# Weight forms and returned chunks of a streaming encoder layer ordered by the scheduler, and other buffer turns in its gate-pair stage

## The chip, the cores and the metric

The kernel runs on one core of a Trainium2 chip. A core has a matrix engine (TensorE, PE in the profile, with PEld for its weight loads), VectorE (DVE), ScalarE (ACT), GpSimd (POOL) and SyncE (SP), whose queue issues most of the transfers. Each engine works through its own list of instructions and waits for others by semaphores. The metric is the time of one execution in microseconds (us); less is better.

## The reference

One layer of a streaming encoder with two parallel mixers, on 2048 prompt rows and 64 new rows of a running stream that has 4096 rows in a cache:

```python
h = rmsnorm(x, norm_g)
q, k, v, ga, u, gb, mg = split(h @ w_in)            # 8 heads of 128; w_in is 1024 x 8192
z = einsum('bqhd,bkhd->bhqk', q, k) * 128 ** -0.5
log_beta = log_sigmoid(z)                           # stick-breaking attention, strictly causal
log_1m = where(mask, log_beta - z, 0)
after = cumsum(log_1m, reverse=True) - log_1m
att = where(mask, exp(log_beta + after), 0) @ v
pb = multi_scale_pool(u) * pool_scale               # trailing means over 2, 4, 8, 16 rows
y_a = (att * silu(ga)) @ w_br_a
y_b = (pb * silu(gb)) @ w_br_b
gate = sigmoid(mg)                                  # 2 x 1024 columns
x = x + (gate[:, :1024] * y_a + gate[:, 1024:] * y_b) @ w_out
y = rmsnorm(x, final_g)                             # returned with k, v and the pool's rows
```

All is float32.

## The kernel before

**Products.** Each float32 operand is split into two parts that TensorE takes fast: `hi` is a rounded copy (a cast on ACT, L91), `lo` is the rest (a subtraction on DVE, L92). A product is three matmuls: hi by hi, hi by lo, lo by hi. So a column slab of 128 weights needs a *form* ahead of its projection (`load_w`): two raw loads of 256 KB by SP (`raw`, three buffers, L310), and two cast-and-subtract pairs into `whi` and `wlo` (two buffers each).

**Attention.** The prompt is worked in two halves of 1024 rows. In the second half, each of the 8 heads (0 to 7) has 28 *units* of 128 query rows by up to 512 key rows. A unit's chain is: scores on PE (L804 to L806), two sigmoids on ACT (`om` L734, `be` L735), for diagonal units a causal select on POOL (L719), a running product from the right on DVE (the scan, L742), the product `be` with it (L745), transposes on PE (`tr`, L818), the split of `tr` into `a` hi and lo (L91, L92), and the products with the values on PE (L833 to L835). Four units make a block; a block's first transpose group reads the `be` of all four. At step n, PE runs the scores of unit n, the transposes of unit n−4 and the products of unit n−5. Between these steps PE works at the four projection slabs (K, V, Q, gate) of the next head, so head 7 has no slabs beside it. The keys and values of the first half come back from memory for each head (`kback`, `vback`) as 2 chunks each, and are split too; each head's own new keys and values are split after their projection (`kst`, `nat`).

**Who sets the order.** PE runs in the order in which the program is written, throughout. ACT, DVE and SP run in written order in the front, in the gate-pair stage and in the closing stage. In the stage of the heads a scheduler orders them, but an instruction given to `keep_in_program_order` stays where the program has it. `placed_split` (L339 to L341) does this for a split. Before, three things in the heads of the second half are placed so: the weight forms, by a hook in the projections that does one half of a form at the 3rd and one at the 6th of every 8 steps (`form_ahead`); the returned chunks, at fixed units (`k` at units 1 and 3, `v` at 7 and 9); and the split of the second own values chunk (`late_v`), at unit 2.

**The gate-pair stage** follows the heads (from L1378 on). Pairs of gate columns are computed by seven products each, p = 0 to 6, on sums of blocks. The accumulators are `z` for even p and `att` for odd p; after p = 0, 2 and 3 the accumulator is copied to `gx` by ACT (`gate_keep`, L1419), and p = 4 overwrites nothing before that copy is done. The weights of the first pair are formed by `stream_forms` (the generator `prepare`, in turns of `whi` and `wlo`), those of later pairs by `pair_forms` from `graw` (loads L1390, differences L1406, L1407, L1411, L1414). Between products runs `weight_sums`, which loads blocks of two other weight matrices by POOL's queue into tiles `ws`, subtracts them and stores the differences (`tw_d`). Its tiles share the buffers of `whi` and `wlo`:

```python
ts = [pool.tile([P, KT, P], F32, name="ws", tag=tag, bufs=2) for tag in ("whi", "wlo")]
```

**The closing stage** computes the two branch products and the output in the same way of seven products. It reads the differences (`wraw<-tw_d`, forms `t1`, `t2`, ...), and the gates that were stored as `sm_d` (`sg<-sm_d`).

Of the kernel before, what the change touches and what calls it, by code (L numbers as in the profile page):

```python
# [8 lines left out]
F32 = mybir.dt.float32  # L9
# [6 lines left out]
P = 128  # L16
# [29 lines left out]
def kernel(  # L46
# [118 lines left out]
    with ExitStack() as front:  # L165
# [161 lines left out]
        def form_w(spare=False):  # L327
            if spare:
                return [attp.tile([P, KT, P], F32R, name=nm, tag="a", bufs=2) for nm in ("wqhi", "wqlo")]
            return [pool.tile([P, KT, P], F32R, name=nm, tag=nm, bufs=2) for nm in ("whi", "wlo")]  # L330
# [5 lines left out]
                split(whi[:, k:k + 4], wlo[:, k:k + 4], raw_w(col, k), eng)  # L336
            return whi, wlo

        def placed_split(hi, lo, src):  # L339
            tc.keep_in_program_order(nc.scalar.copy(hi, src))  # L340
            tc.keep_in_program_order(nc.vector.tensor_tensor(lo, src, hi.bitcast(F32), op=ALU.subtract))  # L341

        cols_ahead, forms_ahead, part_of, steps_of = [], {}, [], [0]

        def form_ahead():
            n = steps_of[0] % 8
            steps_of[0] += 1
            if n == 1 and cols_ahead:
                col = cols_ahead.pop(0)
                forms_ahead[col] = form_w()  # L350
                part_of.extend((forms_ahead[col], k, raw_w(col, k)) for k in range(0, KT, 4))
            elif n in (2, 5) and part_of:
                (hi, lo), k, raw = part_of.pop(0)
                placed_split(hi[:, k:k + 4], lo[:, k:k + 4], raw)

        def proj_ahead(groups, slab):
            col = slab[0]
            yield from proj(groups, [slab], None, [forms_ahead.pop(col)] if col in forms_ahead else (), form_ahead)

        def proj(groups, slabs, eng=None, ws=(), hook=None):  # L360


            ws = list(ws) + [load_w(col, eng, n == 2) for n, (col, _) in enumerate(slabs) if n >= len(ws)]
            for g, (c0, n) in enumerate(groups):
                for (whi, wlo), (_, evac) in zip(ws, slabs):
                    ps = psum.tile([P, 512], F32, name="pj")
                    for k in range(KT):
                        nc.tensor.matmul(ps[:, 0:n], whi[:, k], hhi[:, k, c0:c0 + n], start=k == 0, stop=False)  # L368
                        nc.tensor.matmul(ps[:, 0:n], whi[:, k], hlo[:, k, c0:c0 + n], start=False, stop=False)  # L369
                        nc.tensor.matmul(ps[:, 0:n], wlo[:, k], hhi[:, k, c0:c0 + n], start=False, stop=k == KT - 1)  # L370
                        if k == KT - 1:
                            evac(g, c0, n, ps)
                        if k % 2:
                            if hook:
                                hook()
                            yield 6 * mm_ns(n)

        def groups_of(half):
# [209 lines left out]
                return 107.0  # L588
            defer(2500, rows)

        placed, loaded = {}, {}

        def head_proj(half, hd, fine=False, ws=()):
            groups = groups_of(half)
            col = hd * P
# [34 lines left out]

            def evac_v(g, c0, n, ps):
                st, npr, c, o = staged(g, c0, n, ps)
                late_v = half and not fine and c
                if o == 0 and not late_v:
                    out["v"][c0h + c] = vchunk()

                def rows():
                    r0 = half * 1024 + c0
                    nat = natural(st[:, 0:npr], npr, [vp[r0:r0 + npr, hd, :]])
                    if late_v:  # L640
                        placed.setdefault(hd, []).append((2, out["v"], c0h + c, vchunk, nat))
                    else:
                        vhi, vlo = out["v"][c0h + c]
                        split(vhi[:, o:o + npr], vlo[:, o:o + npr], nat[:, 0:npr], "v" if fine else None)
                    spill("v", c, o, nat[:, 0:npr])
                    if npr < n:
                        later_rows(st[:, npr:n], [vsm[:, hd, :], sv_d[hd]])
                    return npr * 0.85
                defer(6500 if fine else 2500, rows)
# [50 lines left out]
                return  # L700
            if fine:
                yield from proj(FINE_B, [(OFF_K + col, evac_k), (OFF_V + col, evac_v), (OFF_Q + col, evac_q)], None, ws)
                if half:
                    cols_ahead.extend(o + h * P for h in range(1, H) for o in (OFF_K, OFF_V, OFF_Q, OFF_GA))
            else:
                one = proj_ahead if half else lambda groups, slab: proj(groups, [slab])
                yield from one(groups, (OFF_K + col, evac_k))
                yield from one(groups, (OFF_V + col, evac_v))
                yield from one(groups, (OFF_Q + col, evac_q))
            if half:  # L710
                yield from proj_ahead(groups, (OFF_GA + col, evac_g))
            else:
                yield from proj(groups, [(OFF_GA + col, evac_g)])
            heads[half, hd] = out


# [35 lines left out]
        class Stream:  # L752
# [27 lines left out]
            def scores(self, n):  # L780
                hd, qb, c, i = self.units[n]
                out = heads[self.half, hd]
                diag = c == qb
                todo = placed.setdefault(hd, [])
                for cc in range(2 * self.half - 1, -1, -1):
                    if cc in loaded.setdefault(hd, []):
                        continue
                    loaded[hd].append(cc)
                    for kind, chunk in (("k", kchunk), ("v", vchunk)):
                        raw = attp.tile([P, 512], F32, name=f"{kind}back", tag=f"{kind}raw", bufs=2)  # L790
                        nc.sync.dma_start(raw, kvd[kind, hd, cc])
                        todo.append(({"k": 3, "v": 9}[kind] - 2 * cc, out[kind], cc, chunk, raw))
                todo.sort(key=lambda x: x[0])
                while todo and n % 28 >= todo[0][0]:
                    _, of, cc, chunk, raw = todo.pop(0)
                    of[cc] = chunk()
                    placed_split(*of[cc], raw)
                khi, klo = out["k"][c]
                qhi, qlo = out["q"][qb]
                m = P * (i + 1) if diag else 512  # L800
                off = 512 - m
                z = psum.tile([P, 512], F32, name="z")
                qs = slice(i * P, (i + 1) * P)
                nc.tensor.matmul(z[:, off:512], qhi[:, qs], khi[:, 0:m], start=True, stop=False)  # L804
                nc.tensor.matmul(z[:, off:512], qhi[:, qs], klo[:, 0:m], start=False, stop=False)  # L805
                nc.tensor.matmul(z[:, off:512], qlo[:, qs], khi[:, 0:m], start=False, stop=True)  # L806
                om = self.om or self.complements(n)
                be, self.carry[i] = weights_of_block(z, off, om, diag, ahead=lambda: self.prepare(n + 1))
                self.be[hd, qb, c, i] = (be, off)
                return 3 * mm_ns(m) + self.lead(n)  # L810
# [638 lines left out]
        forms_of = pair_forms()  # L1449

        closing_sums = weight_sums()
        next(closing_sums)
        with tc.manual_schedule(engines={E.Activation, E.DVE, E.SP}):
            for c in range(*GATE_PAIRS, 2):
                x = psum.tile([P, 512], F32, name="z")
# [92 lines left out]
        def before_closing():  # L1548
# [32 lines left out]
            for nm, b in (("r21", 0), ("r22", 1)):  # L1581
                for h, t in enumerate(whole_rows(nm, 1, b)):
                    rows(t, 1, b, h)
            yield from todo

        last_gates = [proj(GROUPS_B, [merge_gate(1, c)], ws=ahead_w if c == GATE_PAIRS[1] else ())
                      for c in range(GATE_PAIRS[1], 2 * KT)]
        run((before_closing(), 12.0), (chain(*last_gates), 1.6 * slab_ns(1)))
# [104 lines left out]
    with tc.manual_schedule(engines={E.PE, E.DVE, E.Activation, E.SP}):  # L1693
# [93 lines left out]
        for i, base, nms, at in ((0, 0, WFORMS[3:], [1, 2, 5, 6, 7, 8, 9, 10]),  # L1787
                                 (1, 28, WFORMS, [30 + (8 * h) // 5 for h in range(14)]),
                                 (2, 70, WFORMS[:6], [71 + h for h in range(10)] + [85, 86])):
            when.setdefault(base, []).append((i, nms))  # L1790
            for h in at:
                when.setdefault(h, []).append(None)
        sums_at = {11: 0, 15: 1, 18: 2, 59: 3}
# [9 lines left out]
                pending.append(sums_step(2, sums_at[h]))  # L1803

        pending = []
        wnext = [None]
        for n in range(3):
            load_gate(n)
        for ks in halves:
# [331 lines left out]
```

## Time and profile before

| | before |
|---|---|
| median of 3 runs | 2691.92 us (2687.89 to 2696.8) |
| the profiled execution's own time | 2688.06 us |
| its span (first to last instruction) | 2686.1 us |
| TensorE's granted clock, mean | 0.999 |
| PE busy | 2660.3 us (99%) |
| DVE busy | 1914.1 us (71%) |
| ACT busy | 1327.1 us (49%) |
| POOL busy | 418.2 us (16%) |
| memory traffic over the span | 126 GB/s |

In the rows of the trace the first number is the start in us from the span's start, the second the length in us, then the engine, the line, the operation and its tiles as output<-inputs. A bracket at the end gives the idle time of the engine just before the instruction and what ended it. In a row of the waits the numbers are the total in us, how often, and the longest. The instructions are numbered by the lines of the kernel before; the kernel after has the same code some 30 to 40 lines higher up (the scan L742 is L707, the multiplication L745 is L710).

### The profile page before, as it was taken

The numbers are of one execution on the slowest core, as the hardware profiler recorded it, in microseconds if no ns is written. First come the engines' busy times: TensorE is split into PE (matmuls) and PEld (weight loads), VectorE is DVE, ScalarE is ACT, GpSimd is POOL, SyncE is SP. The second block draws the span as 40 slices with busy tenths as digits, with TensorE's granted clock in tenths as the row PEclk, the third lists the DMA queues.
The fourth block names the chain that finished last, engine by engine and source line by source line (L and its number), as shares of the span: only waits on it lengthen the run. The fifth ranks groups of instructions, "written<-read, shape, count | busy, mean of one in ns | idle before, by whom it ended". The sixth has DMA issues, their size and how long they took to land.

```text
span 2686.1 us, 42384 instructions
## 1 busy us (share of the span) xinstructions
PE 2660.3 (99%) x15066; PEld 2343.0 (87%) x15066; DVE 1914.1 (71%) x3028; ACT 1327.1 (49%) x2627; POOL 418.2 (16%) x1202
## 2 busy tenths in 40 slices
PE   9999999999999999999999999999999999999998
PEld 8999999988899989988888888888887889999886
DVE  5555555567777784488888888888956757677877
ACT  5446444455555553365556656665433443332443
POOL 1122222220000000021212222131000301111001
PEclk9999999999999999999999999999999999999999
DMA  4224222234444444212111211211344868687753
GB/s 149 85 82 131 75 74 74 80 98 153 149 153 152 157 151 157 88 56 60 44 48 55 60 37 55 59 39 49 118 138 148 285 222 297 227 290 249 261 176 119
DMA packets 338706, 342.45 MB, mean 127 GB/s; under 512 B 29799, under 2 KB 281055, under 8 KB 338494
## 3 DMA queue, kind: packets, MB, share of 16 engines
q1 hardware_dynamic: 324382, 293.87, 34.7%
q0 software_dynamic: 14112, 45.89, 4.7%
q8 instruction: 118, 1.93, 0.3%
q14 instruction: 94, 0.77, 0.1%
HBM read 231.02 MB, written 108.65 MB: 126 GB/s over the span
## 4 chain that ended last, share of the span: by engine, by line
PE 90%; DVE 5%; issue 2%; ACT 1%; DMA 1%; POOL 1%; SPq 0%; POOLq 0%; DVEq 0%; ACTq 0%
PE pj L368 15%; PE pj L369 15%; PE pj L370 15%; PE tr L818 4%; PE x L1598 3%; PE x L1600 3%; PE x L1602 3%; PE y L1598 3%; PE y L1600 3%; PE y L1602 3%; PE att L835 2%; PE z L806 2%; DVE om L742 2%; PE z L805 2%; PE att L834 2%
## 5 line engine op out<-in xcount | busy, mean ns | idle before, releaser
L368 PE MATMUL pj<-hhi,whi 128*128 128x256 f32 (+2 forms) x2288 | 817.6, 357 | 0.0
L370 PE MATMUL pj<-hhi,wlo 128*128 128x256 f32 (+2 forms) x2288 | 791.2, 346 | 0.0
L369 PE MATMUL pj<-hlo,whi 128*128 128x256 f32 (+2 forms) x2288 | 790.9, 346 | 0.3 <-DVE hlo L1071 0.3
L742 DVE TENSOR_TENSOR_SCAN om<-om 128x513 f32<-128x513 f32 (+3 forms) x356 | 390.8, 1098 | 200.5 <-POOL om L719 100.3
L370 PEld LDWEIGHTS pj<-hhi,wlo 128*128 128x128 f32 x2288 | 431.2, 188 | 50.6
L368 PEld LDWEIGHTS pj<-hhi,whi 128*128 128x128 f32 x2288 | 432.7, 189 | 46.1 <-ACT hhi L1068 0.3
L369 PEld LDWEIGHTS pj<-hlo,whi 128*128 128x128 f32 x2288 | 432.4, 189 | 44.1 <-DVE hlo L1071 0.5
L734 ACT ACTIVATE om<-z 128x512 f32<-128x512 f32 (+2 forms) x320 | 171.2, 535 | 285.5 <-PE z L806 255.1
L745 DVE TENSOR_TENSOR be<-be,om 128x512 f32<-128x512 f32 (+3 forms) x356 | 218.7, 614 | 33.1 <-POOL carry L744 0.5
L92 DVE TENSOR_TENSOR a<-tr,a 128x512 fp32r<-128x512 f32 (+2 forms) x356 | 215.8, 607 | 27.3 <-ACT a L91 25.2
L91 ACT CAST a<-tr 128x512 fp32r<-128x512 f32 (+2 forms) x356 | 188.0, 528 | 91.7 <-PE tr L818 83.3
L744 POOL COPY carry<-om 128x1 f32<-128x1 f32 x356 | 72.5, 204 | 860.4 <-DVE om L742 834.5
L92 DVE TENSOR_TENSOR wlo<-raw,whi 128x512 fp32r<-128x512 f32 x169 | 115.4, 688 | 96.4 <-ACT whi L91 95.7
L818 PE MATMUL tr<-ident,be 128*128 128x128 f32 x1088 | 174.1, 273 | 7.2 <-DVE be L745 6.6
L818 PEld LDWEIGHTS tr<-ident,be 128*128 128x128 f32 x1088 | 135.9, 140 | 40.7 <-DVE be L745 10.4
L735 ACT ACTIVATE be<-z 128x512 f32<-128x512 f32 (+2 forms) x320 | 169.4, 529 | 0.0
L91 ACT CAST whi<-raw 128x512 fp32r<-128x512 f32 x172 | 106.4, 623 | 95.8 <-PE pj L369 75.0
L833 PE MATMUL att<-a,v 128*128 128x512 f32 (+1 forms) x320 | 132.8, 415 | 0.0
L835 PE MATMUL att<-a,v 128*128 128x512 f32 (+1 forms) x320 | 118.3, 370 | 0.5 <-DVE a L92 0.2
L806 PE MATMUL z<-khi,qlo 128*128 128x512 f32 (+2 forms) x320 | 117.0, 366 | 0.0
L834 PE MATMUL att<-a,v 128*128 128x512 f32 (+1 forms) x320 | 116.4, 364 | 0.0
L805 PE MATMUL z<-klo,qhi 128*128 128x512 f32 (+2 forms) x320 | 116.4, 364 | 0.0
(528 smaller groups left out, 5244.4 us busy)
## 6 DMA issues: line engine op xcount, KB each, us to landing
raw<-in_w_in_dram SPq DMA_DIRECT2D x230, 256.0 KB, 3.0
sg<-sm_d SPq DMA_DIRECT2D x48, 352.0 KB, 5.8
kraw<-in_cache_k_dram SPq DMA_DIRECT2D x64, 256.0 KB, 3.2
vraw<-in_cache_v_dram SPq DMA_DIRECT2D x64, 256.0 KB, 3.1
sm_d<-sgm SPq DMA_DIRECT2D x48, 256.0 KB, 3.3
wraw<-tw_d SPq DMA_DIRECT2D x22, 512.0 KB, 4.0
out_dram<-nat SPq DMA_DIRECT2D x42, 256.0 KB, 2.3
mp_d<-sg POOLq DMA_DIRECT2D x24, 352.0 KB, 4.6
```

The source lines that it names most:

```text
L91: nc.scalar.copy(hi, src)
L92: (nc.gpsimd if eng == "g" else nc.vector).tensor_tensor(lo, src, hi.bitcast(F32), op=ALU.subtract)
L368: nc.tensor.matmul(ps[:, 0:n], whi[:, k], hhi[:, k, c0:c0 + n], start=k == 0, stop=False)
L369: nc.tensor.matmul(ps[:, 0:n], whi[:, k], hlo[:, k, c0:c0 + n], start=False, stop=False)
L370: nc.tensor.matmul(ps[:, 0:n], wlo[:, k], hhi[:, k, c0:c0 + n], start=False, stop=k == KT - 1)
L734: nc.scalar.activation(om[:, off:512], z[:, off:512], AF.Sigmoid, scale=-SCALE)
L742: nc.vector.tensor_tensor_scan(rev, rev, rev, 1.0, op0=ALU.mult, op1=ALU.bypass)
L745: nc.vector.tensor_tensor(be[:, off:512], be[:, off:512], om[:, off + 1:513], op=ALU.mult)
L805: nc.tensor.matmul(z[:, off:512], qhi[:, qs], klo[:, 0:m], start=False, stop=False)
L806: nc.tensor.matmul(z[:, off:512], qlo[:, qs], khi[:, 0:m], start=False, stop=True)
L818: nc.tensor.transpose(tr[:, i * P:(i + 1) * P], be[:, off + j * P:off + (j + 1) * P], ident)
L835: nc.tensor.matmul(self.acc[:, s], vhi[:, js], alo[:, s], start=False, stop=last)
```

## The change

Three things change; no instruction is added or removed, and PE's and POOL's orders stay the same.

1. In the heads of the second half nothing is placed any more. Weight forms go through `load_w` at the start of a slab's projection in the program, the own values are split where they are made, and the returned chunks are split where they are loaded, and the scheduler finds all of them a place.
2. The call `next(closing_sums)` ahead of the pair loop is gone, so each step of `weight_sums` comes one call later, and its first tiles `ws` take their turn of the `whi` and `wlo` buffers after the last form of `stream_forms` instead of before it.
3. The forms of `t1` and what follows it are begun at the end of `before_closing`, so their first two loads of 512 KB stand on SP's queue ahead of the last two gate stores `sm_d<-sgm` and of the first gate loads `sg<-sm_d`.

```diff
-        def placed_split(hi, lo, src):
-            tc.keep_in_program_order(nc.scalar.copy(hi, src))
-            tc.keep_in_program_order(nc.vector.tensor_tensor(lo, src, hi.bitcast(F32), op=ALU.subtract))
...
-        def form_ahead():
-            n = steps_of[0] % 8
...
-            elif n in (2, 5) and part_of:
-                (hi, lo), k, raw = part_of.pop(0)
-                placed_split(hi[:, k:k + 4], lo[:, k:k + 4], raw)
-
-        def proj_ahead(groups, slab):
...
-        def proj(groups, slabs, eng=None, ws=(), hook=None):
+        def proj(groups, slabs, eng=None, ws=()):
...
                 def rows():
                     r0 = half * 1024 + c0
                     nat = natural(st[:, 0:npr], npr, [vp[r0:r0 + npr, hd, :]])
-                    if late_v:
-                        placed.setdefault(hd, []).append((2, out["v"], c0h + c, vchunk, nat))
-                    else:
-                        vhi, vlo = out["v"][c0h + c]
-                        split(vhi[:, o:o + npr], vlo[:, o:o + npr], nat[:, 0:npr], "v" if fine else None)
+                    split(vhi[:, o:o + npr], vlo[:, o:o + npr], nat[:, 0:npr], "v" if fine else None)
...
-                        todo.append(({"k": 3, "v": 9}[kind] - 2 * cc, out[kind], cc, chunk, raw))
-                todo.sort(key=lambda x: x[0])
-                while todo and n % 28 >= todo[0][0]:
-                    _, of, cc, chunk, raw = todo.pop(0)
-                    of[cc] = chunk()
-                    placed_split(*of[cc], raw)
+                        out[kind][cc] = chunk()
+                        split(*out[kind][cc], raw)
...
         closing_sums = weight_sums()
-        next(closing_sums)
         with tc.manual_schedule(engines={E.Activation, E.DVE, E.SP}):
...
             yield from todo
-
+            wnext[0] = forms(0, WFORMS[3:], True)
+            next(wnext[0])
+
+        wnext = [None]
...
-            when.setdefault(base, []).append((i, nms))
+            if i:
+                when.setdefault(base, []).append((i, nms))
```

Where the orders differ, on DVE, at three places. In the rows the names are `om` (the scan's tile), `be`, `a`, `klo` and `v` (lo parts of chunks), `wlo` (lo part of weights), `qlo`; a number behind a name is the tile's.

The first place: DVE in a steady head, from unit 2's scan to unit 3's multiplication. Before:

```order
L742 SCALAR_TENSOR_TENSOR om_15806<-om_15806 128x385
L745 TENSOR_TENSOR be_15838<-be_15838,om_15806 128x384
L92 TENSOR_TENSOR a_15856<-tr_15851,a_15856 128x512
L89 CAST khi_15870<-kst_15868 128x512
L92 TENSOR_TENSOR klo_15871<-kst_15868,khi_15870 128x512
L341 TENSOR_TENSOR klo_15875<-kback_15740,khi_15874 128x512
L742 SCALAR_TENSOR_TENSOR om_15845<-om_15845 128x513
L92 TENSOR_TENSOR a_15900<-tr_15895,a_15900 128x512
L745 TENSOR_TENSOR be_15882<-be_15882,om_15845 128x512
```

After:

```order
L707 SCALAR_TENSOR_TENSOR om_15813<-om_15813 128x385
L710 TENSOR_TENSOR be_15840<-be_15840,om_15813 128x384
L92 TENSOR_TENSOR a_15858<-tr_15853,a_15858 128x512
L89 CAST khi_15872<-kst_15870 128x512
L92 TENSOR_TENSOR klo_15873<-kst_15870,khi_15872 128x512
L707 SCALAR_TENSOR_TENSOR om_15847<-om_15847 128x513
L92 TENSOR_TENSOR a_15898<-tr_15893,a_15898 128x512
L710 TENSOR_TENSOR be_15880<-be_15880,om_15847 128x512
```

The subtraction of the returned keys has left the place ahead of unit 3's scan.

The second place: DVE in the same head, around units 22 to 24. Before:

```order
L92 TENSOR_TENSOR a_16598<-tr_16595,a_16598 128x256
L341 TENSOR_TENSOR wlo_16577<-raw_16578,whi_16576 128x512
L742 SCALAR_TENSOR_TENSOR om_16589<-om_16589 128x513
L92 TENSOR_TENSOR a_16627<-tr_16625,a_16627 128x128
L745 TENSOR_TENSOR be_16616<-be_16616,om_16589 128x512
L742 SCALAR_TENSOR_TENSOR om_16619<-om_16619 128x513
L745 TENSOR_TENSOR be_16637<-be_16637,om_16619 128x512
L682 TENSOR_TENSOR sga_16652<-pj_16539,sga_16652 128x512
L92 TENSOR_TENSOR a_16660<-tr_16655,a_16660 128x512
```

After:

```order
L92 TENSOR_TENSOR a_16595<-tr_16592,a_16595 128x256
L707 SCALAR_TENSOR_TENSOR om_16586<-om_16586 128x513
L92 TENSOR_TENSOR a_16622<-tr_16620,a_16622 128x128
L710 TENSOR_TENSOR be_16611<-be_16611,om_16586 128x512
L92 TENSOR_TENSOR klo_16764<-kback_16761,khi_16763 128x512
L707 SCALAR_TENSOR_TENSOR om_16614<-om_16614 128x513
L653 TENSOR_TENSOR sga_16647<-pj_16542,sga_16647 128x512
L710 TENSOR_TENSOR be_16632<-be_16632,om_16614 128x512
L92 TENSOR_TENSOR v_16254<-nat_16284,v_16254 128x512
L92 TENSOR_TENSOR a_16655<-tr_16650,a_16655 128x512
```

A weight subtraction has left, and a keys' subtraction of the next head and the own values' subtraction now stand ahead of the last `a`.

The third place: DVE in head 0, units 22 and 23. Before:

```order
L742 SCALAR_TENSOR_TENSOR om_14466<-om_14466 128x513
L745 TENSOR_TENSOR be_14493<-be_14493,om_14466 128x512
L92 TENSOR_TENSOR qlo_14509<-pj_14405,qhi_14508 128x512
L92 TENSOR_TENSOR a_14515<-tr_14512,a_14515 128x256
L742 SCALAR_TENSOR_TENSOR om_14496<-om_14496 128x513
L745 TENSOR_TENSOR be_14525<-be_14525,om_14496 128x512
L92 TENSOR_TENSOR a_14543<-tr_14541,a_14543 128x128
```

After:

```order
L707 SCALAR_TENSOR_TENSOR om_14459<-om_14459 128x513
L710 TENSOR_TENSOR be_14486<-be_14486,om_14459 128x512
L92 TENSOR_TENSOR wlo_14737<-raw_14738,whi_14736 128x512
L92 TENSOR_TENSOR qlo_14502<-pj_14400,qhi_14501 128x512
L92 TENSOR_TENSOR a_14508<-tr_14505,a_14508 128x256
L707 SCALAR_TENSOR_TENSOR om_14489<-om_14489 128x513
L92 TENSOR_TENSOR wlo_14737<-raw_14742,whi_14736 128x512
L710 TENSOR_TENSOR be_14518<-be_14518,om_14489 128x512
L92 TENSOR_TENSOR a_14546<-tr_14544,a_14546 128x128
```

Two weight subtractions of the next head now stand in unit 23's chain, one ahead of `qlo` and one between scan and multiplication.

More of the change, by code (lines that the diff above doesn't have):

```diff
@@ L337, in load_w @@
             return whi, wlo
-        def placed_split(hi, lo, src):
-            tc.keep_in_program_order(nc.scalar.copy(hi, src))
-            tc.keep_in_program_order(nc.vector.tensor_tensor(lo, src, hi.bitcast(F32), op=ALU.subtract))
-        cols_ahead, forms_ahead, part_of, steps_of = [], {}, [], [0]
-        def form_ahead():
-            n = steps_of[0] % 8
[L347 to L351, printed above, removed]
-            elif n in (2, 5) and part_of:
-                (hi, lo), k, raw = part_of.pop(0)
-                placed_split(hi[:, k:k + 4], lo[:, k:k + 4], raw)
-        def proj_ahead(groups, slab):
-            col = slab[0]
-            yield from proj(groups, [slab], None, [forms_ahead.pop(col)] if col in forms_ahead else (), form_ahead)
-        def proj(groups, slabs, eng=None, ws=(), hook=None):
+        def proj(groups, slabs, eng=None, ws=()):
             ws = list(ws) + [load_w(col, eng, n == 2) for n, (col, _) in enumerate(slabs) if n >= len(ws)]
@@ L373, in proj @@
                         if k % 2:
-                            if hook:
-                                hook()
                             yield 6 * mm_ns(n)
@@ L589, in later_rows @@
             defer(2500, rows)
-        placed, loaded = {}, {}
         def head_proj(half, hd, fine=False, ws=()):
@@ L632, in evac_v @@
                 st, npr, c, o = staged(g, c0, n, ps)
-                late_v = half and not fine and c
-                if o == 0 and not late_v:
+                if o == 0:
                     out["v"][c0h + c] = vchunk()
+                vhi, vlo = out["v"][c0h + c]
                 def rows():
@@ L702, in head_proj @@
                 yield from proj(FINE_B, [(OFF_K + col, evac_k), (OFF_V + col, evac_v), (OFF_Q + col, evac_q)], None, ws)
-                if half:
-                    cols_ahead.extend(o + h * P for h in range(1, H) for o in (OFF_K, OFF_V, OFF_Q, OFF_GA))
-            else:
[L706 to L713, printed above, removed]
+            else:
+                yield from proj(groups, [(OFF_K + col, evac_k)])
+                yield from proj(groups, [(OFF_V + col, evac_v)])
+                yield from proj(groups, [(OFF_Q + col, evac_q)])
+            yield from proj(groups, [(OFF_GA + col, evac_g)])
             heads[half, hd] = out
@@ L783, in scores @@
                 diag = c == qb
-                todo = placed.setdefault(hd, [])
                 for cc in range(2 * self.half - 1, -1, -1):
-                    if cc in loaded.setdefault(hd, []):
+                    if cc in out["k"]:
                         continue
-                    loaded[hd].append(cc)
                     for kind, chunk in (("k", kchunk), ("v", vchunk)):
@@ L1805 @@
         pending = []
-        wnext = [None]
         for n in range(3):
```

## The prediction

> **What bounds the kernel now.** I read the page's busy times first, then what ended TensorE's waits, then single stretches in order of time.
>
> ```profile
> span 2686.1 us, 42384 instructions
> ...
> PE 2660.3 (99%) x15066; PEld 2343.0 (87%) x15066; DVE 1914.1 (71%) x3028; ACT 1327.1 (49%) x2627; POOL 418.2 (16%) x1202
> ```
>
> TensorE (PE) is busy for 2660.3 of 2686.1 us, so all of its idle time is 25.8 us. Its work and order stay as they are, so no edit here can gain more than 25.8. A loss has no such lid: every late input becomes idle time.
>
> The waits of PE come next: us in total, times, longest.
>
> ```profile
> PE tr L818 <- DVE be L745: 6.6, 11, 1.5
> PE z L1230 <- ACT gx L1419: 3.0, 1, 3.0
> ...
> PE att L1230 <- ACT whi L91: 0.5, 1, 0.5
> ```
>
> The first row is in the attention: a transpose waits for the weights `be` that VectorE (DVE) multiplies at L745. The other two stand in the pair stage, once each. The change touches both. The stretches of one steady head of the second half, of the last head and of the first follow.
>
> ```profile
> 1600.10:1693.50 93.40, 92.76 (x478) 76.95 (x477) 76.88 (x106) 55.99 (x113) 21.24 (x74) 1.00 0.17 52
> 1787.00:1870.00 83.00, 80.85 (x408) 66.36 (x407) 71.05 (x98) 49.19 (x98) 21.19 (x68) 1.00 0.16 51
> 1137.00:1226.00 89.00, 88.45 (x450) 72.53 (x449) 74.31 (x102) 52.64 (x106) 19.20 (x74) 1.00 0.17 51
> ```
>
> The columns are the length, then busy time of PE, weight load, DVE, ScalarE (ACT) and GpSimd (POOL), then the granted clock. In a steady head PE idles 0.64 us of 93.4, while DVE is busy for 76.9: 16.5 us are free on DVE, but it matters where they lie. Only every fourth unit's multiplication is urgent, because a block's first transpose needs the `be` of all four of its units. There are six steady heads.
>
> **The change part by part.** *Steady heads, unit 3.* One head, in order of time:
>
> ```profile
> 1322.32 0.30 POOL L719 TENSOR_SCALAR_AFFINE_SELECT om<-om 128x128 f32<-128x128 f32 x1 [2.69 <-ACT om L734]
> ...
> 1328.04 0.62 ACT L340 CAST khi<-kback 128x512 fp32r<-128x512 f32 x1
> ...
> 1328.56 0.59 ACT L734 ACTIVATE om<-z 128x512 f32<-128x512 f32 x1
> ...
> 1328.60 0.69 DVE L92 TENSOR_TENSOR klo<-kst,khi 128x512 fp32r<-128x512 f32 x1
> ...
> 1329.21 0.68 DVE L341 TENSOR_TENSOR klo<-kback,khi 128x512 fp32r<-128x512 f32 x1
> 1329.22 0.82 POOL L719 TENSOR_SCALAR_AFFINE_SELECT om<-om 128x128 f32<-128x128 f32 x1 [1.28 <-ACT om L734]
> ...
> 1330.08 1.29 DVE L742 TENSOR_TENSOR_SCAN om<-om 128x513 f32<-128x513 f32 x1 [0.19 <-POOL om L719]
> ...
> 1331.88 0.68 DVE L745 TENSOR_TENSOR be<-be,om 128x512 f32<-128x512 f32 x1
> ...
> 1332.61 0.33 PE L818 MATMUL tr<-ident,be 128*128 128x128 f32 x1 [0.63 <-DVE be L745]
> ```
>
> The chain into the transpose that waits 0.63 is: ACT `om`, POOL select, DVE scan, DVE multiplication. The change takes the cast of the returned keys (0.62 of sequence on ACT, 0.52 between the two starts 1328.04 and 1328.56) and its subtraction (two starts on DVE 0.61 apart) out of this place. With `om` about 0.5 earlier, the select starts about 0.5 earlier; it still meets `klo<-kst`, which holds DVE to 1329.29. A select beside no such subtraction took 0.30 (1322.32), the one here 0.82. So the scan starts at about 1329.5 in place of 1330.08, and the wait of 0.63 nearly goes. I take −0.55 per head, between 0 (the select is as late as now) and −0.75 (the idle time with the slow restart behind it). Six heads: −3.3, ends 0 and −4.5. What is late next is the scan behind its `om`, with no margin to spare.
>
> The row for the select is where a rule bears: the Trainium skill, SBUF — State Buffer, section "SBUF: two separate sides", says that DVE reading two SBUF inputs and GpSimd share a port by an exclusive lock, and that the one that loses is blocked fully. By that rule the select waits until `klo<-kst` ends and the gain stays 0.55; with no lock it would be the 0.75. The trace agrees with the lock, 0.82 against 0.30.
>
> *Steady heads, unit 24.* The subtractions that left unit 3 and its neighbour now stand late in the head before. The same order, at this place before:
>
> ```profile
> 1398.84 1.22 DVE L742 TENSOR_TENSOR_SCAN om<-om 128x513 f32<-128x513 f32 x1
> ...
> 1400.16 0.69 DVE L745 TENSOR_TENSOR be<-be,om 128x512 f32<-128x512 f32 x1
> ...
> 1401.37 0.68 DVE L92 TENSOR_TENSOR a<-tr,a 128x512 fp32r<-128x512 f32 x1
> ...
> 1402.48 0.40 PE L835 MATMUL att<-a,v 128*128 128x512 f32 x1
> ```
>
> Now one `klo` and one `v` subtraction stand ahead of `a`, at 0.6 each: 1.2 later. Before, `a` ends at 1402.05 and PE needs it at 1402.48, 0.43 of margin. The cost is 1.2 − 0.43 = 0.77; I take 0.7, since one weight subtraction leaves just ahead of it, between 0 (the scan waits for its `om` anyway and the `klo` hides in that wait) and 1.2. Six heads: +4.2, ends 0 and +7.2. The ACT casts of both pieces move along and hide under ACT's 40% of free time.
>
> *The weight forms.* They now stand as pairs of subtractions in four places per head in place of eight single ones. Where one is urgent, at unit 7:
>
> ```profile
> 1343.81 0.69 DVE L745 TENSOR_TENSOR be<-be,om 128x512 f32<-128x512 f32 x1
> ...
> 1345.85 0.60 PE L818 MATMUL tr<-ident,be 128*128 128x128 f32 x4
> ```
>
> `be` ends at 1344.50 and PE comes at 1345.85: 1.35 of margin. One more subtraction of 0.6 leaves 0.75, two leave 0.15. I cost this at 0; the cover is that margin, and the slower rival below is the case without it. Net of the steady heads: −3.3 + 4.2 = +0.9. The raw weight loads are issued earlier or later by some units on SP; their landing is not on the path (PE never waits for `whi` in a head).
>
> *First head.* Two stretches, in order of time:
>
> ```profile
> 1154.82 0.30 PE L818 MATMUL tr<-ident,be 128*128 128x128 f32 x1 [0.31 <-DVE a L92]
> ...
> 1207.10 0.69 DVE L745 TENSOR_TENSOR be<-be,om 128x512 f32<-128x512 f32 x1
> ...
> 1207.85 0.14 PEld L818 LDWEIGHTS tr<-ident,be 128*128 128x128 f32 x1 [0.34 <-DVE be L745]
> ```
>
> At unit 23 PE already waits 0.34 for `be`, so there is no margin, and two weight subtractions now stand in the chain ahead of it: +1.2. At unit 6 one more stands ahead of the `a` that PE already waits 0.31 for: +0.6. That is 1.8; I take +1.7, between 0 and 3.
>
> *Last head.*
>
> ```profile
> 1809.89 0.67 DVE L341 TENSOR_TENSOR v<-vback,v 128x512 fp32r<-128x512 f32 x1
> ...
> 1810.48 0.68 DVE L745 TENSOR_TENSOR be<-be,om 128x512 f32<-128x512 f32 x1
> ...
> 1811.21 0.33 PE L818 MATMUL tr<-ident,be 128*128 128x128 f32 x1 [1.52 <-DVE be L745]
> ```
>
> The subtraction for the returned values stands between scan and multiplication and leaves: 0.6 for itself and about 0.3 for its cast on ACT: −0.9, ends 0 and −1.5 (the whole wait).
>
> *Pair stage.* In order of time:
>
> ```profile
> 2053.69 0.99 SPq L1390 DMA_DIRECT2D graw<-in_w_in_dram  x2
> ...
> 2057.11 0.59 ACT L1419 COPY gx<-z 128x512 f32<-128x512 f32 x1 [2.11 <-PE z L1232]
> ...
> 2062.28 0.62 ACT L91 CAST whi<-raw 128x512 fp32r<-128x512 f32 x1 [4.58 <-PE z L1231]
> ...
> 2062.95 0.50 PE L1230 MATMUL att<-s1hi,whi 128*128 128x512 f32 x1 [0.48 <-ACT whi L91]
> ...
> 2068.61 0.58 ACT L1419 COPY gx<-z 128x512 f32<-128x512 f32 x1
> ...
> 2069.24 0.50 PE L1230 MATMUL z<-s3hi,fhi 128*128 128x512 f32 x1 [3.00 <-ACT gx L1419]
> ```
>
> Without the early step of the weight sums, the last weight form of the stage before takes the free turn of `whi`, not one that product p=2 still reads. Its cast no longer waits 4.58 and can run at about 2057.7, behind `gx`. The work queued behind it moves up by the same 4.6, unless the weights `graw` are late: three DVE subtractions (1.9 by three starts 0.6 apart), the cast of the first `fhi`, and then the second `gx`. The loads of `graw` are issued at 2053.69, and their way took
>
> ```profile
> DMA to landing us min/median/max: 4.2/5.6/9.6
> ```
>
> At the median they land at about 2060, and `gx` of p=2 ends at about 2065.0. PE was through with p=3 at 2069.24 − 3.00 = 2066.24; without the 0.48 and its slow restart it comes to p=4 at about 2065.3, after `gx`. So both waits go, 3.48, and their restarts (the first product behind each shows 0.50 for the 0.40 at 1402.48; with those behind it I estimate 0.2 each): −3.9. Ends: −4.3, with twice the restarts, and −1 with `graw` at 9.6, where the chain starts at 2063.3 as now and only the 0.48 and its restart go. The sums themselves come one step later, on DVE and on POOL's queue. I cost that at 0: their four steps and the pair's seven products meet in every alignment already before, and in the whole kernel PE's only waits in this stage are the two above. Without that cover a sum ahead of a form costs 0.6, the price of a subtraction.
>
> *Closing.* Two loads of 512 KB (t1) stand on SP's queue ahead of the last gate stores and of the first gate loads.
>
> ```profile
> 2197.05 1.23 DVE L1529 TENSOR_TENSOR t2lo<-wraw,t2hi 128x1024 fp32r<-128x1024 f32 x1 [1.35 <-ACT t2hi L1528]
> ...
> 2201.50 0.89 DVE L1720 TENSOR_TENSOR s<-r,r 128x704 f32<-128x704 f32 x1 [3.22 <-DMA sm_d<-sgm]
> ...
> 2206.82 1.82 DVE L92 TENSOR_TENSOR rlo<-r,rhi 128x704 fp32r<-128x704 f32 x2
> ...
> 2209.76 0.32 PE L1598 MATMUL x<-rhi,t2hi 128*128 128x352 f32 x1
> ```
>
> The t1 loads need the buffers that the forms of t2 read until 2198.28 and hold the store behind them by about 1.5; `s` starts at about 2203, `rlo` ends at about 2210.2 in place of 2208.64, and PE comes at 2209.76: +0.4. I take +0.3, between 0 and 1.5.
>
> The sum is +0.9 + 1.7 − 0.9 − 3.9 + 0.3 = −1.9. The profiled execution took 2688.06 (its span 2686.1 and 2 around it), which gives 2686.2. It lies 3.9 below the median of 2691.92, and single runs spread from 2687.89 to 2696.8; on the median's footing the forecast is 2690.
>
> **The rivals.**
>
> *The pair stage gains nothing.* `graw` lands late, or another buffer turn is the late one. The median of 5.6 speaks against it, the 9.6 for it. −3.9 goes to −1 or 0: about 2694.
>
> *The heads gain, too.* The wait at unit 24 hides in the scan's wait for `om`, unit 3 gives the whole 0.75: −4.5 + 0.5 for unit 24 − 3.9 and the rest +1: about 2685.
>
> *Slower: the paired weight subtractions don't fit.* If a pair falls ahead of an urgent scan or product (units 27 and 0, 6, 13, 20), each place can cost 0.6. Four places in six heads are +14.4, and with the forecast's −1.9 this ends at 2704. It decides once a place has under 0.6 of margin where the second subtraction stands; at unit 7 the 1.35 speaks against it, at unit 24 the 0.43 shows that such margins exist.
>
> *The change does nothing in the heads.* The order is moved, but DVE's 16.5 us of free time take all of it: +0.9 and +1.7 go, which leaves −4.5, about 2687.
>
> **How the numbers follow.** Forecast (2690, its own range 2687 to 2693) 0.45; nothing in the heads 0.15; the pair stage gains nothing 0.18; the heads gain 0.10; slower 0.12. The range goes from 2682, the heads' gain with both bounds favourable, to 2702, into the slower rival, which leaves about 0.1 above and 0.05 below. Two medians of this kernel can be told apart from about 0.3%, 8 us. The forecast and three rivals lie within that, so "same" gets 0.84; faster, which needs −8 of 25.8 us of idle time, 0.05; slower, most of the fourth rival, 0.11.
>
> **What would show it.** Right: PE's row "tr L818 <- DVE be" (by its new line) drops from 6.6 at unit 3 and in the last head and gets new entries in the first head; an entry "att L835 <- DVE a" of about 0.7 in six heads; no wait of PE for `whi` or `gx` at the pair stage's start; `s` in the closing stage at about 2203 less what was gained ahead of it. A steady head is then 93.5 long. Wrong: a steady head over 95 (the pairs don't fit), a wait of PE for `gx` that stays near 3, or idle time of PE in the pair stage that follows the sums' later steps.

## The result and the profile after

| | before | after |
|---|---|---|
| median | 2691.66 us (12 runs, 2687.79 to 2696.8) | 2686.76 us (12 runs, 2684.28 to 2689.01) |
| profiled execution, own time | 2688.06 us | 2686.66 us |
| its span | 2686.1 us | 2684.8 us |

The ratio after to before is 0.9984 (95% interval 0.9976 to 0.9992): 4.3 us faster, between 2.2 and 6.5, by that ratio. The two profiled executions differ by only 1.4 us. Where the other 3 us are is the second half of this study. Among the executions behind runs 1 to 4, one of run 2 and one of the kernel before took 5356 us, twice as long as all others; the ratios leave them out, and without them the medians of run 2 and of that kernel before are 2692.98 and 2691.38, in place of 2693.48 and 2691.43.

The page after, and what ended the waits of PE (total in us, times, longest; the scores' line is now L765, the transposes' L777, the last product's L794, the gate pairs' L1189, the closing stage's L1561):

```profile
span 2684.8 us, 42398 instructions
...
PE 2663.0 (99%) x15066; PEld 2345.2 (87%) x15066; DVE 1916.2 (71%) x3028; ACT 1325.1 (49%) x2627; POOL 421.6 (16%) x1202
```

```profile
PE att L794 <- DVE a L92: 2.6, 7, 0.4
PE tr L777 <- DVE be L710: 2.6, 6, 0.9
...
PE x L1561 <- DVE rlo L92: 1.3, 1, 1.3
```

The wait for `be` fell from 6.6 to 2.6, a wait for `a` came in with 2.6, the two waits of the pair stage are gone, and one of 1.3 for `rlo` stands in the closing stage. PE is also 2.7 us longer *busy* with the same instructions: each engine has as many busy ones as before (the 14 more of the total are none of these).

PE's order is the same in both kernels, so the start of each matmul can be set against that of the same matmul before. The difference jumps at single places, and lies flat between them:

| place | jump, us | forecast |
|---|---|---|
| front, up to 1130 (nothing is changed there; −0.7 in a second profile of the kernel after) | −1.2 | 0 |
| head 0, units 6 and 23 | −0.2, +0.9 | +0.6, +1.2 |
| unit 3 of a steady head (six) | −0.6 to −0.8 | −0.55 |
| unit 24 of a steady head (six) | +0.6 to +0.7 | +0.7 |
| one place in the third steady head, at 1465 | +0.2 | 0 |
| last head | −1.0 | −0.9 |
| start of the pair stage | −4.3 | −3.9 |
| closing stage, first products | +1.6 | +0.3 |
| closing stage, to its end | +2.1, evenly | 0 |

One steady head after (the one shown of before), in order of time, at unit 3:

```profile
1327.64 0.60 ACT L699 ACTIVATE om<-z 128x512 f32<-128x512 f32 x1 [0.16 <-PE z L765]
...
1328.11 0.69 DVE L92 TENSOR_TENSOR klo<-kst,khi 128x512 fp32r<-128x512 f32 x1
1328.31 0.65 POOL L684 TENSOR_SCALAR_AFFINE_SELECT om<-om 128x128 f32<-128x128 f32 x1 [1.02 <-ACT om L699]
...
1328.99 1.29 DVE L707 TENSOR_TENSOR_SCAN om<-om 128x513 f32<-128x513 f32 x1 [0.19 <-POOL om L684]
```

And at unit 24:

```profile
1397.68 0.68 DVE L92 TENSOR_TENSOR klo<-kback,khi 128x512 fp32r<-128x512 f32 x1
...
1398.28 1.21 DVE L707 TENSOR_TENSOR_SCAN om<-om 128x513 f32<-128x513 f32 x1
...
1400.00 0.68 DVE L710 TENSOR_TENSOR be<-be,om 128x512 f32<-128x512 f32 x1
1400.60 0.68 DVE L92 TENSOR_TENSOR v<-nat,v 128x512 fp32r<-128x512 f32 x1
...
1401.20 0.68 DVE L92 TENSOR_TENSOR a<-tr,a 128x512 fp32r<-128x512 f32 x1
...
1401.93 0.50 PE L794 MATMUL att<-a,v 128*128 128x512 f32 x1 [0.41 <-DVE a L92]
```

At unit 3 the select follows `om` and still takes 0.65, beside the subtraction that remains; the scan starts 1.1 earlier, of which 0.5 is the lead that this execution has on the other by then. At unit 24 both pieces stand where the order had shown them, and PE waits 0.41 for `a`.

The pair stage after:

```profile
2055.98 0.59 ACT L1378 COPY gx<-z 128x512 f32<-128x512 f32 x1 [2.11 <-PE z L1191]
...
2056.46 0.62 ACT L91 CAST whi<-raw 128x512 fp32r<-128x512 f32 x1
...
2062.90 0.58 ACT L1378 COPY gx<-z 128x512 f32<-128x512 f32 x1
...
2063.89 0.39 PE L1189 MATMUL z<-s3hi,fhi 128*128 128x512 f32 x1
```

The cast of `whi` follows `gx` at once, the second `gx` ends at 2063.48, 0.4 before PE reaches p = 4, and no matmul waits.

The closing stage after:

```profile
2190.62 3.53 SPq L1480 DMA_DIRECT2D wraw<-tw_d  x2
...
2194.20 0.94 SPq L369 DMA_DIRECT2D sm_d<-sgm  x2
...
2199.66 0.89 DVE L1681 TENSOR_TENSOR s<-r,r 128x704 f32<-128x704 f32 x1 [5.90 <-DMA sm_d<-sgm]
...
2205.92 0.43 PE L1561 MATMUL x<-rlo,t2hi 128*128 128x352 f32 x1 [1.32 <-DVE rlo L92]
```

The t1 loads hold SP's queue until 2194.20, and `s` waits 5.90 where it waited 3.22. This suggests that the t1 loads cost the 1.6; run 3 tests it.

### The profile page after: what moved, and what is told of

The parts are those of the page before. It is cut to its first block, busy times and chain, and to the rows that moved or that the text cites. A ratio compares the mean times of both kernels' runs of the same rounds, so it can differ in the third digit from the quotient of the medians.

```text
span 2684.8 us, 42398 instructions
## 1 busy us (share of the span) xinstructions
PE 2663.0 (99%) x15066; PEld 2345.2 (87%) x15066; DVE 1916.2 (71%) x3028; ACT 1325.1 (49%) x2627; POOL 421.6 (16%) x1202
## 4 chain that ended last, share of the span: by engine, by line
PE 92%; DVE 4%; ACT 1%; DMA 1%; issue 1%; POOL 0%; SPq 0%; DVEq 0%; ACTq 0%; POOLq 0%
PE pj L347 15%; PE pj L349 15%; PE pj L348 15%; PE tr L777 4%; PE x L1559 3%; PE x L1563 3%; PE x L1561 3%; PE att L794 2%; PE y L1563 2%; PE y L1559 2%; PE y L1561 2%; PE z L765 2%; PE att L793 2%; PE att L792 2%; PE z L764 2%; PE z L763 2%
## 5 line engine op out<-in xcount | busy, mean ns | idle before, releaser
L92 DVE TENSOR_TENSOR wlo<-raw,whi 128x512 fp32r<-128x512 f32 x225 | 154.1, 687 | 98.7 <-ACT whi L91 98.1
L91 ACT CAST whi<-raw 128x512 fp32r<-128x512 f32 x228 | 141.1, 625 | 100.2 <-PE pj L348 83.8
L777 PE MATMUL tr<-ident,be 128*128 128x128 f32 x1088 | 174.1, 273 | 3.3 <-DVE be L710 2.6
L777 PEld LDWEIGHTS tr<-ident,be 128*128 128x128 f32 x1088 | 135.9, 140 | 36.8 <-DVE be L710 6.1
L794 PE MATMUL att<-a,v 128*128 128x512 f32 (+1 forms) x320 | 119.0, 372 | 2.9 <-DVE a L92 2.6
L765 PE MATMUL z<-khi,qlo 128*128 128x512 f32 (+2 forms) x320 | 116.9, 365 | 0.0
```

Source lines behind the costliest of these rows:

```text
L92: (nc.gpsimd if eng == "g" else nc.vector).tensor_tensor(lo, src, hi.bitcast(F32), op=ALU.subtract)
L777: nc.tensor.transpose(tr[:, i * P:(i + 1) * P], be[:, off + j * P:off + (j + 1) * P], ident)
L794: nc.tensor.matmul(self.acc[:, s], vhi[:, js], alo[:, s], start=False, stop=last)
```

## The experiments

Times with a ratio were measured against the kernel before on the same chip; a time without a ratio is that of a single execution, so there the waits in its profile carry the argument and not the time. Jumps are differences of matmul starts as in the table above, against the first profile of before.

**1. The dropped call alone.**

```diff
         closing_sums = weight_sums()
-        next(closing_sums)
```

> Only the call ahead of the pair loop is dropped; heads and closing stay as before. Theory (the parts add up, each with its own mechanism): the two waits of PE at the start of the pair stage (0.48 and 3.00) go, 4.3 us with their restarts, and nothing else changes, since the loads of t1 stand where they stood: about 2687.3 against 2691.7, no wait of PE for rlo in the closing stage. Rival (the closing stage's inputs arrive when memory lets them, and whoever comes there earlier waits there): PE comes 4.3 earlier, waits 1.3 for rlo at the same place as in the changed kernel, and the gain is about 2.8: 2688.9.

2684.19 against 2691.43, ratio 0.9974 (0.9964 to 0.9983). Both pair waits go (−4.3), yet among the waits of PE one for `rlo` stands in the closing stage, with t1 where it was:

```profile
PE y L1599 <- DVE rlo L92: 2.2, 1, 2.2
```

So the t1 loads aren't needed for such a wait: the rival is right on that, though not on the place and the length. On the time both are wrong: the medians differ by 7 us, more than the 4.3.

**2. The heads alone.** Part 1 of the change, without parts 2 and 3.

> Only the order in the heads is left to the scheduler; pair stage and closing as before. Theory: in each of six steady heads the wait at unit 3 goes (-0.63) and one at unit 24 for the a of VectorE comes (+0.65), which cancel; head 0 costs 0.7, the last head gains 1.0: -0.3 in all, about 2691.4, with both pair waits (0.48, 3.00) still there. Rival (part of the 4.9 that the medians of the changed kernel gained is from the heads, which one profile does not show): 2 to 3 us faster, about 2689.

2693.48, ratio 1.0007 (0.9998 to 1.0017): the heads bring no gain. The jumps are those of the changed kernel to 0.1 (unit 3 −0.6, unit 24 +0.65, head 0 −0.2 and +0.95, last head −1.0), 0.0 from the first head to the last. The 3.0 stays in the pair stage, with 1.6 more of loss behind it.

**3. The change without the early t1 loads.** Part 3 undone.

> The changed kernel with the loads of t1 put back to the closing stage. Theory (these loads hold up the last gate stores on SP's queue): the wait of PE for rlo, 1.3, goes with its restart, s in the closing stage is no more than 0.5 later against PE than before, and the time is 1.5 below the changed kernel: 2685.2. Rival (PE is just early there): the wait of 1.3 stays, 2686.8. The matmuls of the closing stage, 0.1589 apart before and 0.1600 after (0.7% over some 300 us, 2.1 us in all), go back to 0.1589 if the early loads caused that, and take either value if it belongs to the execution.

2685.88, ratio 0.9981 (0.9972 to 0.9989), no different from the changed kernel.

```profile
PE y L1558 <- DVE rlo L92: 1.3, 1, 1.3
```

```profile
2197.27 0.89 DVE L1678 TENSOR_TENSOR s<-r,r 128x704 f32<-128x704 f32 x1 [3.06 <-DMA sm_d<-sgm]
```

The wait is as long as before, but at the first product with t1 instead of t2, and `s` starts 2.4 earlier than in the changed kernel (2197.27 against 2199.66). So the early loads do hold up the gate stores, as the theory says, and without them t1 is late instead. On the time the rival is right: the early loads move the wait and cost nothing net that these times can show.

**4. The returned chunks elsewhere.** On the kernel before with the call dropped:

```diff
-todo.append(({"k": 3, "v": 9}[kind] - 2 * cc, out[kind], cc, chunk, raw))
+todo.append(({("k", 1): 1, ("k", 0): 5, ("v", 1): 8, ("v", 0): 10}[kind, cc], out[kind], cc, chunk, raw))
```

> The kernel before with the call ahead of the pair loop dropped, and with the returned chunks placed elsewhere: keys at units 1 and 5 (before 1 and 3), values at 8 and 10 (before 7 and 9). Weight forms and own values placed as before. Theory (the waits at units 3 and 7 are due to the chunk pieces placed there, and nothing pays for the move): -0.63 in six heads, -1.0 in the last, -4.3 in the pair stage: -9.1, about 2682.6. Rival (the pieces cost the same wherever they stand, as unit 24 did for the scheduler): new waits at units 6 or 11 of about 0.6 in six heads, and -5.3 in all, 2686.4.

2679.41, ratio 0.9954 (0.9942 to 0.9967). The jumps are −0.6 to −0.8 at unit 3 of six heads, −1.0 in the last, and nothing comes at units 6 or 11: 4.8 of heads. The theory of the place holds, and the whole is again faster, by some 3 us, than the sum that the theory had made of its parts.

**5 and 6. Turn or step.** The dropped call does two things: the sums come a step later, and their first tiles take another turn. The first run keeps the steps and changes the turn, the second the reverse.

```diff
                     if c == GATE_PAIRS[0]:
                         next(prepare, None)
+                        if p == 0:
+                            next(closing_sums)
```

> The kernel before with the first call of the weight sums moved from ahead of the pair loop to behind the last form of the stage before (first product of the first pair): the sums run at the steps of before, and only the turns of the whi and wlo buffers are those of the changed kernel. Theory (the turn is the cause): whi<-raw goes right behind gx, and PE's waits of 0.48 and 3.00 at the start of the pair stage go, 4.3 us with their restarts, as in the run with the call dropped. Rival (the later step of the sums frees VectorE or the queues): the two waits stay, 3.5 us.

```diff
-                    if c > GATE_PAIRS[0] or p > 2:
+                    if c > GATE_PAIRS[0] or p > 3:
                         next(closing_sums, None)
```

> The kernel before with the first call kept ahead of the pair loop, and the second one (at the fourth product of the first pair) left out: every sum runs one step later, and the turns of the buffers stay those of before. Theory (the turn is the cause): PE's waits of 0.48 and 3.00 stay. Rival (the later step is the cause): both go, 4.3 us.

2682.42 for the turn and 2691.53 for the step, beside 2691.88 for the kernel before. In the first, no wait of PE for `whi` or `gx` is left at the start of the pair stage (a jump of −4.4). In the second, by its rows in order of time, the cast still waits, and so does PE:

```profile
2061.51 0.62 ACT L91 CAST whi<-raw 128x512 fp32r<-128x512 f32 x1 [4.58 <-PE z L1231]
...
2068.47 0.80 PE L1230 MATMUL z<-s3hi,fhi 128*128 128x512 f32 x1 [3.00 <-ACT gx L1419]
```

With the turn alone the waits go, with the step alone they stay: the turn of the buffers is the cause, the step is not.

**7 and 8. Which piece makes the wait at unit 24.** On the changed kernel, the returned keys are placed again (at units 1 and 5), and in the other run the own values (at unit 2):

```diff
+                        if kind == "k":
+                            todo.append((5 - 4 * cc, out[kind], cc, chunk, raw))
```

> The changed kernel with the split of the returned keys placed again, at units 1 and 5; the scheduler then sets the own values' split behind the a of unit 24 instead of ahead of it. Theory (two pieces ahead of a cost 1.2 less its margin of 0.43): the waits for a at unit 24 go, 0.65 in six heads, and unit 3 stays without a wait: 3.9 below the changed kernel's heads. Rival (each piece costs wherever it stands): new waits at units 1 and 5, no gain.

```diff
+                    if late_v:
+                        placed.setdefault(hd, []).append((2, out["v"], c0h + c, vchunk, nat))
```

> The changed kernel with the own values' split placed at unit 2 again. Ahead of the a at unit 24 then stands one piece, the keys', and a returned chunk of values behind it. Theory (pieces of 0.6 against a margin of 0.43): 0.2 is left of the 0.65 per head. Rival 1 (the keys' piece hides in the scan's wait, the own values made it all): 0. Rival 2 (the keys' piece ahead of the scan made it all): 0.65 stays.

From the end of head 0 to the end of the last steady head, the changed kernel loses 0.3 on the kernel before, the keys' run gains 2.6 and the values' run 3.7. With the keys placed, unit 24 has no wait; about 0.25 per head comes at about unit 6, and one head has a wait of 0.31 for another `a`, so the rival holds for a part. With the values placed the price of unit 24 is gone altogether: the number of the first rival. Its rows at unit 24:

```profile
1397.27 0.68 DVE L92 TENSOR_TENSOR klo<-kback,khi 128x512 fp32r<-128x512 f32 x1
...
1399.59 0.67 DVE L720 TENSOR_TENSOR be<-be,om 128x512 f32<-128x512 f32 x1
1400.19 0.68 DVE L92 TENSOR_TENSOR a<-tr,a 128x512 fp32r<-128x512 f32 x1
...
1400.95 0.47 PE L810 MATMUL att<-a,v 128*128 128x512 f32 x1
```

The keys' piece is still ahead of the scan, and it does not hide in a wait of the scan, as the first rival had it: the scan follows it without a pause. But `sga`, which stood between `be` and `a` before, now runs between the scan and `be`, so `a` follows `be` directly. It ends at 1400.87, 0.08 ahead of PE, where the margin was 0.43 before: the piece delays `a` by 0.35 against PE, not by its full 0.6, which is what the theory had charged. The own values' 0.6 on top of that is more than the margin. Those values alone, without the keys ahead of the scan, were not run.

**9 and 10. The two kernels once more.** Nothing edited.

> The kernel before once more, for a second profile. Two things differed among the profiles that no edit explains: the distance of the closing stage's matmuls (0.1589 us in the first profile of before, 0.1589 to 0.1612 in the others) and a wait of PE for rlo there (none in the first profile of before, 0 to 2.2 in the others). Theory (both belong to the execution): at least one of the two takes another value here. Rival (both belong to the kernel): 0.1589 and no wait again.

> The changed kernel once more, for a second profile. Theory (the wait for rlo in the closing stage hangs on when loads and gate stores land, which differs from execution to execution): another wait than 1.3, between 0 and 2.5, and another distance than 0.1600. Rival (SP's queue order makes it): 1.3 at the same matmul again. The heads and the pair stage repeat to 0.1 us by either.

The second profile of before has an own time of 2692.61, 4.6 above the first, and its heads are the same to 0.2. It differs at two places, both of which follow a wait of PE. One window each, 2068 to 2072 in the pair stage and 2222 to 2225 in the closing stage, first in the first profile and then in the second (the third number from the end is the granted clock):

```profile
2068.00:2072.00 4.00, 2.76 (x12) 2.30 (x13) 2.27 (x4) 2.81 (x6) 0.44 (x1) 1.00 0.85 269
2222.00:2225.00 3.00, 3.00 (x20) 3.00 (x20) 1.62 (x2) 1.09 (x2) 0.00 (x0) 1.00 0.84 297
```

```profile
2068.00:2072.00 4.00, 3.23 (x8) 2.62 (x9) 2.68 (x4) 2.34 (x5) 0.00 (x0) 0.57 0.88 209
2222.00:2225.00 3.00, 3.00 (x12) 3.00 (x11) 3.00 (x3) 0.54 (x1) 0.00 (x0) 0.50 0.84 243
```

In the pair stage both wait 3.00 for `gx`; the second execution then works on at about half clock and loses 1.4 more. In the closing stage the first execution has no wait at all; the second has the wait shown here, behind which the clock falls to 0.50, and the two together cost 3.6:

```profile
2220.35 0.43 PE L1600 MATMUL y<-rlo,t1hi 128*128 128x352 f32 x1 [1.75 <-DVE rlo L92]
```

The load of t1 releases the first cast of `t1hi` at 2212.60 there, where it was 2209.41 in the first profile, while PE is only 0.9 later. So whether there is a wait for `rlo` differs from execution to execution; it comes with the kernel before, too. The changed kernel's second profile has it at the same matmul as its first, but 0.6 long instead of 1.3.

The other difference belongs, as far as two profiles each can say, to the kernel. The windows from 2260 to 2460 show how many matmuls PE did in 200 us of the closing stage (in the brackets behind PE's busy time). The first profile of before:

```profile
2260.00:2460.00 200.00, 200.00 (x1260) 200.00 (x1260) 145.81 (x135) 64.56 (x62) 28.08 (x42) 1.00 0.78 259
```

Its second profile:

```profile
2260.00:2460.00 200.00, 200.00 (x1261) 200.00 (x1260) 145.17 (x135) 66.57 (x64) 29.21 (x45) 1.00 0.77 256
```

The changed kernel's first profile:

```profile
2260.00:2460.00 200.00, 200.00 (x1252) 200.00 (x1251) 145.15 (x134) 64.94 (x63) 27.79 (x43) 1.00 0.77 259
```

Its second:

```profile
2260.00:2460.00 200.00, 200.00 (x1252) 200.00 (x1251) 145.12 (x134) 64.71 (x63) 27.83 (x42) 1.00 0.78 260
```

The heads alone (run 2):

```profile
2260.00:2460.00 200.00, 200.00 (x1243) 200.00 (x1242) 143.18 (x132) 64.42 (x62) 27.27 (x41) 1.00 0.76 254
```

The mean distances are 0.1589, 0.1600 and 0.1611 us at a clock of 1.00, and in all fourteen profiles there is no fourth value. Over the some 2000 matmuls a step is about 2.1 us: that is 2.1 of the 2.7 by which PE is longer busy after.

**11 and 12. Faster versions.** On the kernel of run 4: the call moved as in run 5, instead of dropped; or the t1 loads behind the last gate store and ahead of the first gate load.

```diff
-        wnext = [None]
+        wnext = [forms(0, WFORMS[3:])]
+        next(wnext[0])
         for n in range(3):
             load_gate(n)
```

> The kernel with the returned chunks at units 1, 5, 8 and 10, and with the first call of the weight sums moved behind the last form instead of dropped, so that the sums run at the steps of before. Theory (the turn alone counts, and a step of the sums changes nothing): 2679.4 as with the call dropped. Rival (sums that end a step later delay what the closing stage loads): no wait for rlo, about 1 us less, 2678.4.

> The kernel with the returned chunks at units 1, 5, 8 and 10 and the call dropped, and with the loads of t1 on SP's queue behind the last gate store, ahead of the first gate loads. Theory (the wait of 0.6 for rlo at the first product with t1 comes of late loads of t1): it goes, 0.9 with its restart, 2678.5. Rival (these loads then hold up others): 2679.4 or more, with a wait at a product with t2.

2680.94, ratio 0.9956 (0.9944 to 0.9969), and 2679.55, ratio 0.9951 (0.9937 to 0.9964). The first has a wait of 1.1 for `rlo`, so sums that end earlier don't prevent it. The second has none in its profile, but its time isn't distinguishable from that of run 4. Run 4 and these two beat both kernels, by 12 to 14 us on before.

## Why the prediction was right

The forecast of 2690 in a range of 2682 to 2702 took in 2686.76, a change of 0.2% and so within the 0.3% that the forecast called the same. It is the wide range that did this: the sum of −1.9 is less than half of the 4.3 to 4.9 that were measured, and 2686.76 lies just outside the forecast's own 2687 to 2693. By its number the rival "nothing in the heads" (2687) comes nearer, but that is luck: the waits in the heads did move as forecast, and only their sum is 0.0. Step by step:

- *Unit 3* was right in place and size (−0.6 to −0.8 for −0.55), and the select's 0.65 beside `klo<-kst` is what was assumed. The Trainium skill (SBUF — State Buffer, "SBUF: two separate sides") would have the select blocked whole; here the select starts 0.20 into the subtraction and ends 0.16 behind it, with 0.65 in place of the undisturbed 0.30. That agrees for the most part: less than its 0.30 is left behind the subtraction.
- *Unit 24* was right in size (+0.6 to +0.7 for +0.7). The working, 1.2 less a margin of 0.43, has two errors that cancel, so the size is in part luck: the delay is 0.95, since the keys' piece costs `a` only 0.35 (run 8), and alone it is free; and the 0.52 that this leaves beyond the margin grows by some 0.1 to the loss of 0.6 to 0.7, for the release and the slow restart, which this term left out.
- *The weight forms* in pairs cost nothing in steady heads; the slower rival didn't come.
- *Head 0* was mis-sized: +0.7 for +1.7. The term at unit 23 is +0.9 for +1.2. The one at unit 6 came out as −0.2. The returned keys' subtraction leaves unit 3 of head 0 as well, for which the forecast has no term: −0.6 at 1144 to 1150. At 1153 PE then waits 0.65 for the `a` for which it waited 0.31, +0.3. Run 4, which leaves the weight forms where they were, has 0.77 there, so PE's earlier arrival is enough for this wait.
- *Last head*: −1.0 for −0.9.
- *Pair stage*: −4.3 for −3.9, and the cause is the one named (runs 5 and 6). The term that was mis-sized is the price of the restarts, put at 0.2 each. The waits are 3.48 and the jump is −4.3, so they took 0.4 each even at full clock. And in three of the four profiles that have the wait for `gx` (before again, heads alone, the step alone; 2.98 to 3.00 in all) the granted clock fell and another 1.4 to 1.6 were lost; the profile that the forecast was made from is the fourth. In those three the waits and what followed them are worth about 5.7.
- *Closing stage*: the step that failed is "t1 loads hold the gate stores, +0.3". They hold them by 2.4 (run 3), not 1.5. And `s` was expected to move up by all that was gained ahead of it: in run 3 PE comes 5.1 earlier and `s` only 4.2. But run 3 has a wait as long without the early loads, and the kernel before has one of 1.75 in its second profile: there was little margin before the change either, and the loads land at other times in each execution. The slower distance of the matmuls, +2.1, was not foreseen.

The sum was −1.9, and about −4.9 between the medians was measured. If most executions of the kernel before have the dip of the clock in the pair stage (−5.7), then with the heads at 0.0, the matmuls' distance at +2.1, and jumps in the closing stage of 0 and 3.6 in two profiles before against 1.6 and 0.9 in two after, one comes to −2 to −6. The shares of the last two in the medians aren't settled.

It also fits the footing. The first profiled execution, which had neither dip nor closing wait, lies 3.6 below the median of the twelve; the second, with both, lies 0.9 above it. What the unprofiled executions had isn't known.

## What to carry to other kernels

Read from the order what stands directly ahead of the instruction that the bottleneck waits for, and hold it against that instruction's margin: here one piece of 0.6 used 0.35 of a margin of 0.43, and a second made the wait. Count the turns of a shared pool of buffers: here a tile that was taken one call too early made a cast wait 4.58 for a buffer while the other was handed to work that needed it later. And where a stall of the matrix engine goes, count with its aftermath, and take a second profile before you price it.

## What the runs showed of the hardware

- *The clock after short waits.* After a wait of 2.98 to 3.00 us the granted clock over 2068 to 2072 was 1.00 in one execution and 0.57, 0.64 and 0.57 in three; after one of 1.75 it was 0.50 over 3 us, and behind those of 2.2 in runs 1 and 7 it stayed at 1.00. The Trainium skill (TensorE: Matmul & The Clock Gate, "Part 1: The HAM clock gate (the "warmup" mystery)") tells of a window of about 3.4 us that runs free of the program, and half rate after an idle one. The traces agree with the half rate, and that the same wait is followed by a dip in one execution and not in another fits a window that runs free; they also show that waits of 3.00 and of 1.75 can be enough.
- *Three distances of the same matmuls.* The closing stage's 128x352 matmuls start 0.1589, 0.1600 or 0.1611 us apart in the mean at a granted clock of 1.00, the same in two profiles of the same kernel (two kernels were profiled twice). What sets it stays open: small edits far from that stage change it (run 6 against before), and run 3's other executions, up to 5.5 us below its profiled one, are faster than its wait of 1.3 alone explains, so that it may change with the execution too; that is not shown.
